# Two 512-token projections in the two banks of one accumulator, and the low tile of the next step made first

## The chip, the core and the metric

The kernel runs on one core of a Trainium2 chip. The metric is device microseconds (us) of one execution, the median over runs. Five engines work side by side and wait for each other through semaphores: TensorE (PE) multiplies matrices into the accumulators of PSUM, VectorE (DVE), ScalarE (ACT) and GpSimd (POOL) work element by element, and SyncE (SP) issues the DMAs.

## The reference

Two layers of a block with three parallel mixers run over 512 latent tokens and 256 context tokens; the context only feeds the latent tokens, and is not updated in the last layer. Cut to what matters:

```python
def _layer(x, ctx, ..., update_ctx):
    h  = _rms_norm(x, norm_g)   * (1.0 + scale)   + shift
    hc = _rms_norm(ctx, norm_g) * (1.0 + scale_c) + shift_c
    (ga_q, ga_k, ga_v, ga_g, ga_lr, hg_q, hg_f, hg_i, hg_g,
     wa_q, wa_k, wa_v, wa_g, mg) = _split_in(jnp.matmul(h, w_in))
    ...                                   # the same columns of hc @ w_in
    y_gla = _head_norm_gate(o_gla, ...)   # chunked recurrence, both directions
    y_hg  = _head_norm_gate(o_hg, ...)    # another one
    y_att = _window_attention(q, k, v, kc, vc, attn_sink) * jax.nn.silu(wa_g)
    x_new = x + gate * _merge((y_gla, y_hg, y_att), mg, w_branch, w_out)
    if update_ctx:                        # layer 0 only
        ctx = ctx + gate_c * _merge(...)
```

`_merge` projects each branch to 1024 columns, weights it with a sigmoid gate, sums the three and multiplies by `w_out`.

## The kernel before

Activations lie transposed, 128 channels to a tile (8 tiles, kt or k), tokens along the columns: 512 latent, then 256 context. Each is split into a rounded high part (hH) and the rest (hL), the weights likewise into WH and WL in a ring `wring` of three slots, and one output block of 128 columns is the sum of WH·hH, WH·hL and WL·hH over the 8 tiles: 24 matmuls of 512 columns, and 24 of 256 where the context is needed (`proj_T`). In layer 0 every projection has both; in layer 1 only keys, forget gates and values need the context, so queries, gates, branch and output projections have 512 columns alone.

A projection's result stands in a tile `acc` of [128, 1024] in PSUM, that is two banks of 512; the pool has two such tiles, taken in turn by `acc()`. Behind the projection an instruction of ScalarE or VectorE reads the tile out (for rotary queries five do: four copies and one product). Smaller results use `mx`, four tiles of one bank.

The recurrences and attention blocks run as background generators. `Emit` keeps an estimated time for each engine, and `pace()` puts background steps between the matmuls of a projection as long as VectorE and ScalarE are less than `SLACK` (3000 ns by its estimate) ahead of TensorE. So what an estimate says of an accumulator (`ps_tile`, `free_at`) decides where background work stands. The order of each engine is the order in which the program records it.

At the very beginning (`j_start`, layer 0) eight rounds k run: `make_h2(k)` makes hL of tile k on VectorE; `products(k, js=(0,))` uses tile k for the first of two projections; `cond_mm(k+2)` multiplies the conditioning weights; `products(k, js=(1,))`; `cond_cols(k+2)` turns the conditioning product by 2-column matmuls into columns, which VectorE adds up; `make_h1(k+2)` scales tile k+2 on VectorE and makes its hH on ScalarE. From round 3 on a weight split for the next job (`split_v`) follows.

Of the kernel before, what the change touches and what calls it, by code (L numbers as in the profile page):

```python
# [28 lines left out]
KT = 8  # L29
NL = 512  # L30
# [289 lines left out]
class Emit:  # L320
# [144 lines left out]
    def stt(self, out, a, s, b, op0, op1):  # L465
        self.nc.vector.scalar_tensor_tensor(out, a, s, b, op0=op0, op1=op1)  # L466
        self._do('v', 1.04 * self.size(out) + 65, out, [a, s, b])
# [5 lines left out]
    def copy(self, out, in_, eng='va', psum=False):  # L473
        n = self.size(out)
        cost = {'v': (1.04 if psum else 0.52) * n + 65, 'a': 0.833 * n + 70, 'g': 3.34 * n + 260}
        cost = {k: c for k, c in cost.items() if k in eng and not (psum and k == 'g')}
        e = self._pick(cost, out, [in_])
        if e == 'v':
            self.nc.vector.tensor_copy(out, in_)  # L479
        elif e == 'a':  # L480
            self.nc.scalar.copy(out, in_)  # L481
        else:
            self.nc.gpsimd.tensor_copy(out, in_)  # L483
        self._do(e, cost[e], out, [in_])
# [47 lines left out]
    def mm(self, out, lhsT, rhs, start=True, stop=True):  # L532
        self.nc.tensor.matmul(out, lhsT=lhsT, rhs=rhs, start=start, stop=stop)  # L533
        n = self.size(rhs)
        if rhs.dtype == F32:
            cost = max(1.667 * n + 6, 224)
        elif rhs.dtype == BF16:
            cost = 60
        else:
            cost = max(0.4167 * n + 13.5, 107 if self.size(lhsT) > 64 else 60)  # L540
        self._do('pe', cost, out, [lhsT, rhs])
# [17 lines left out]
def build(nc, tc, A, COL, es, dump=None):  # L559
# [50 lines left out]
    def ps_tile(kind, p, shape, n):  # L610
        t = p.tile(shape, F32, tag=kind, name=kind)
        names = live[kind]
        if len(names) >= n:
            old = min(names, key=lambda x: E.seq.get(x, 0))
            E.free_at[t.tensor.name] = E.used.get(old, 0.0) + E.FREE
            names.remove(old)
        names.append(t.tensor.name)
        return t

    def mx():  # L620
        return ps_tile('mx', mx_p, [P, 512], 4)

    def acc():
        return ps_tile('acc', acc_p, [P, 1024], 2)


    queue = arena.queue = deque()
# [66 lines left out]
    def pace(slack=SLACK):  # L694
        while max(E.t['v'], E.t['a']) < E.t['pe'] + slack:
            b = first(E.t['pe'] + 50)
            if b is None:
                break
            step(b)
# [91 lines left out]
    def ahead():  # L791

        splits(at_job[0] + NS)

    def WH(i):
        return wring[:, i % NS, 1]

    def WL(i):
        return wring[:, i % NS, 0]

    def proj_T(i, xH, xL, ctx, m=P):

        ps = acc()
        E.t['pe'] = max(E.t['pe'], wready[i])
        for t0, n in ((0, NL), (NL, NC)) if ctx else ((0, NL),):
            k = 0
            for kt in range(KT):
                for w, x in ((WH(i), xH), (WH(i), xL), (WL(i), xH)):
                    mm(ps[0:m, t0:t0 + n], w[:, kt, 0:m], x[kt][:, t0:t0 + n],
                       start=(k == 0), stop=(k == 3 * KT - 1))  # L810
                    k += 1
                if kt == 1 and t0 == 0:
                    ahead()
                if kt % 2 == 1:
                    pace()
        pace()
        return ps
# [114 lines left out]
    def make_h1(l, k, x, r, parts=(0, 1)):  # L932

        for j in parts:
            sl = slice(PARTS[j][0], sum(PARTS[j]))
            stt(x.ap[:, sl], x.ap[:, sl], amod[l][:, k, j:j + 1], r.ap[:, sl], ALU.mult, ALU.mult)
        for j in parts:
            sl = slice(PARTS[j][0], sum(PARTS[j]))
            act(hH[k][:, sl], x.ap[:, sl], AF.Identity, bias=ada[l][:, k, j:j + 1], scale=1.0)

    def make_h2(l, k, x, parts=(0, 1)):

        for j in parts:
            sl = slice(PARTS[j][0], sum(PARTS[j]))
            stt(hL[k][:, sl], x.ap[:, sl], ada[l][:, k, j:j + 1], hH[k][:, sl].bitcast(F32), ALU.add, ALU.subtract)
        if 1 in parts:
            x.free()
# [420 lines left out]
    def split_v():  # L1368
        raw = raw_v.pop(0)
        hl = [arena.alloc(576, True) for _ in range(2)]  # L1370
        E.split(hl[0].r, hl[1].r, raw.ap)
        raw.free()
        S0.setdefault('wvl', []).append([b.r.rearrange("p (a b) -> p a b", b=288) for b in hl] + hl)

    def j_start(l, arg):

        begin_layer(l)
        xs = x_in[l]
# [3 lines left out]
        def load_rest():  # L1382
            for d in range(2):
                nc.sync.dma_start(out=wz_raw[d].ap[0:96], in_=A['wa2'][l][:, d])
            if l > 0:
                return
            S0['mask'] = mb = arena.alloc(6 * P)
            nc.sync.dma_start(out=mb.ap, in_=A['mask'])
            nc.sync.dma_start(out=rot, in_=A['rot'])
# [22 lines left out]
        def cond_mm(k):  # L1412


            w = stage[k]
            ps = mx()
            for kt in range(KT):
                j = kt % 4
                E.mm4(ps[32 * j:32 * j + 32, 0:2 * P], cs32[:, kt], w[kt // 3].ap[:, 256 * (kt % 3):256 * (kt % 3 + 1)],
                      start=(kt < 4), stop=(kt >= 4))  # L1420
            stage[k] = r = arena.alloc(NT)
            copy(r.ap[:, 0:2 * P], ps[:, 0:2 * P], eng='va', psum=True)
            for b in w:
                b.free()

        def cond_cols(k):

            r = stage.pop(k)
            pt = mx()
            for j in range(2):  # L1430
                mm(pt[:, 2 * j:2 * j + 2], r.ap[:, P * j:P * (j + 1)], sel)
            r.free()
            two = ada[l][:, k:16:8]
            tt(two, pt[:, 0:4].rearrange("p (a b) -> p a b", b=2),
               cols_at(f'b_ada{l}', k, 16, 8).unsqueeze(2).to_broadcast([P, 2, 2]), ALU.add)
            stt(amod[l][:, k], ada[l][:, 8 + k], 1.0, col(f'norm_g{l}', k).to_broadcast([P, 2]), ALU.add, ALU.mult)
# [18 lines left out]
        else:  # L1455
            load_rest()
            rs = S0['rs']
            ada_mod(l, 0, 8)
            i = take(2)
        ps = [acc(), acc()]  # L1460
        parts = [((0, NL), (NL, NC)), ((0, NL), (NL, NC))[:2 if S_['ctx'] else 1]]

        def products(kt, of=(0, 1), js=(0, 1)):
            E.t['pe'] = max(E.t['pe'], wready[i + 1])
            for j in js:
                for w, x in ((WH(i + j), hH), (WH(i + j), hL), (WL(i + j), hH)):
                    for t0, n in parts[j]:
                        if (t0 > 0) not in of:
                            continue
                        c = count[j][t0 > 0]  # L1470
                        mm(ps[j][:, t0:t0 + n], w[:, kt], x[kt][:, t0:t0 + n], start=(c == 0), stop=(c == 3 * KT - 1))
                        count[j][t0 > 0] += 1

        count = [[0, 0], [0, 0]]
        if l == 0:

            for k in range(KT):
                make_h2(l, k, xs[k])
                if k == 1:
                    load_rest()  # L1480
                if k == KT - 1:
                    ahead()
                products(k, js=(0,))
                if k + 2 < KT:
                    cond_mm(k + 2)
                products(k, js=(1,))
                if k + 2 < KT:
                    cond_cols(k + 2)
                    make_h1(l, k + 2, xs[k + 2], rs)
                if k >= 3 and raw_v:  # L1490
                    split_v()
        else:

            tail = S0.pop('tail')
            for part in range(2):
                make_h1(l, 0, xs[0], rs, (part,))
                if part == 0:
                    tail[0]()
                for k in range(KT):
                    if k + 1 < KT:  # L1500
                        make_h1(l, k + 1, xs[k + 1], rs, (part,))
                    make_h2(l, k, xs[k], (part,))
                    if part and k == KT - 1:
                        ahead()
                    products(k, (part,))
                    if part == 0 and k in (0, 2):
                        tail[1 + k // 2]()
# [49 lines left out]
    def j_gk(l, h):  # L1557
        ps = proj_T(take(), hH, hL, True)
        S_['k'][h] = kb = arena.alloc(NT)
        copy(kb.ap, ps[:, 0:NT], eng='va', psum=True)  # L1560
# [298 lines left out]
```

## Time and profile before

| what | value |
|---|---|
| median of 3 runs | 2699.06 us (2696.78 to 2701.8) |
| the profiled execution | 2699.6 us, its span 2697.8 us |
| TensorE busy | 2617.0 us, 97% of the span |
| VectorE, ScalarE, GpSimd busy | 1767.1, 1105.6, 168.9 us |
| granted clock of TensorE, mean | 0.991 |
| DMA | 227.68 MB, 84 GB/s |

Busy times are united over an engine's instructions. A matmul's row runs on a little after the next has begun, so rows of TensorE overlap. A bracket behind a row of the timeline gives the idle time before it and the instruction whose end ended it. Names are without numbers: `s` stands for any of 40 slots, `mx` and `acc` for any of the tiles in PSUM. Layer 0 ends near 1540 us.

### The profile page before, as it was taken

To read this page: it belongs to the slowest core of one execution; us is meant where nothing else is said; L and a number is where in the kernel's file an instruction comes from. 1 tells how busy PE (TensorE), PEld (TensorE's weight loads), DVE (VectorE), ACT (ScalarE), POOL (GpSimd) and SP (SyncE) were. 2 spreads that over 40 slices of the span, in tenths; PEclk is the share of its full clock that TensorE was granted. 3 is DMA by queue.
4 is the path that set the end of the run, shared out by engine and by line. 5 is a ranking of instruction groups with operands and counts; after the bars stand their busy time and mean duration, and the time that the engine had idled before them with its cause. 6 is when DMAs were issued, how large, how long until landed. Compare 5 with 4: busy or idle time off the path is not lost. (4 is left out here: it accounts for less than half of the span.)

```text
span 2697.8 us, 40579 instructions
## 1 busy us (share of the span) xinstructions
PE 2617.0 (97%) x15982; PEld 2318.4 (86%) x15982; DVE 1767.1 (66%) x3592; ACT 1105.6 (41%) x2037; POOL 168.9 (6%) x426
## 2 busy tenths in 40 slices
PE   6999999999999999999999999999999999999998
PEld 3899988999888889888888898888899797888886
DVE  4466666786877766775556556667887887765454
ACT  3444434443434455411111344444665545563222
POOL 0000002010020100000000000001011110000000
PEclk8999999999999999999999999999999999999999
DMA  6111121111121112463423411112221122224333
GB/s 251 40 50 57 59 67 59 50 52 57 49 66 50 46 57 74 148 204 101 140 95 102 141 55 56 62 63 63 69 65 62 55 75 73 73 87 142 126 125 109
DMA packets 89342, 227.68 MB, mean 84 GB/s; under 512 B 9920, under 2 KB 30912, under 8 KB 89152
## 3 DMA queue, kind: packets, MB, share of 16 engines
q1 hardware_dynamic: 89152, 225.09, 25.3%
q8 instruction: 126, 2.06, 0.3%
q14 instruction: 64, 0.52, 0.1%
HBM read 202.24 MB, written 22.81 MB: 83 GB/s over the span
## 5 line engine op out<-in xcount | busy, mean ns | idle before, releaser
L533 PE MATMUL acc<-hH,wring 128*128 128x512 f32 (+1 forms) x5040 | 1402.9, 357 | 14.9 <-ACT s L439 9.8
L533 PEld LDWEIGHTS acc<-hH,wring 128*128 128x128 f32 x5040 | 897.7, 190 | 143.1 <-ACT s L439 11.6
L533 PE MATMUL acc<-hL,wring 128*128 128x512 f32 (+1 forms) x2520 | 884.8, 352 | 16.9 <-DVE hL L466 16.8
L533 PEld LDWEIGHTS acc<-hL,wring 128*128 128x128 f32 x2520 | 479.1, 190 | 76.9 <-DVE hL L466 20.5
L533 PE MATMUL mx<-s,s 128*128 128x256 f32 (+4 forms) x2576 | 389.5, 299 | 12.9 <-DVE s L513 4.4
L533 PEld LDWEIGHTS mx<-s,s 128*128 128x128 f32 (+1 forms) x2576 | 348.4, 192 | 32.8 <-issue 7.1
L450 DVE TENSOR_TENSOR wring<-raw,wring 128x1024 fp32r<-128x1024 f32 x269 | 330.7, 1235 | 28.2 <-ACT wring L481 19.3
L533 PE MATMUL acc<-s,wring 128*128 128x512 f32 (+1 forms) x1728 | 332.4, 354 | 0.5 <-DVE s L450 0.5
L533 PEld LDWEIGHTS acc<-s,wring 128*128 128x128 f32 x1728 | 285.6, 189 | 46.4 <-DVE s L450 0.9
L439 ACT ACTIVATE s<-s 128x768 f32<-128x768 f32 (+1 forms) x321 | 259.0, 816 | 129.8 <-DVE s L466 83.1
L481 ACT CAST wring<-raw 128x1024 fp32r<-128x1024 f32 x173 | 179.7, 1048 | 276.9 <-PE acc L533 182.9
L533 PE MATMUL acc<-wring,hH 128*128 128x256 f32 x1536 | 286.1, 285 | 0.0
L450 DVE TENSOR_TENSOR s<-s,s 128x768 f32<-128x768 f32 (+5 forms) x279 | 234.0, 855 | 67.0 <-ACT s L439 45.9
L533 PEld LDWEIGHTS acc<-wring,hH 128*128 128x128 f32 x1536 | 242.2, 192 | 0.3
L533 PE MATMUL acc<-wring,hL 128*128 128x256 f32 x768 | 217.2, 283 | 0.0
L450 DVE TENSOR_TENSOR s<-s,fb 128x128 f32<-128x128 f32 (+2 forms) x608 | 183.0, 361 | 0.8
L439 ACT ACTIVATE s<-acc 128x768 f32<-128x768 f32 (+2 forms) x112 | 76.3, 683 | 255.9 <-PE acc L533 236.2
L481 ACT COPY s<-mx 128x256 f32<-128x256 f32 (+2 forms) x190 | 67.4, 379 | 225.8 <-PE mx L533 142.8
L479 DVE CAST wring<-raw 128x1024 fp32r<-128x1024 f32 x103 | 71.6, 695 | 117.5 <-PE acc L533 114.4
L533 PEld LDWEIGHTS acc<-wring,hL 128*128 128x128 f32 x768 | 147.3, 192 | 0.2
L481 ACT COPY s<-acc 128x768 f32<-128x768 f32 (+2 forms) x129 | 87.8, 681 | 101.0 <-PE acc L533 98.9
L549 PE MATMUL mx<-const,s 128*128 128x128 f32 (+1 forms) x732 | 109.1, 275 | 15.7 <-DVE s L450 14.6
(112 smaller groups left out, 2144.8 us busy)
## 6 DMA issues: line engine op xcount, KB each, us to landing
raw<-in_W SPq DMA_DIRECT2D x308, 512.0 KB, 3.8
y<-s SPq DMA_DIRECT2D x80, 128.0 KB, 1.7
s<-y SPq DMA_DIRECT2D x24, 384.0 KB, 6.1
s<-in_xT SPq DMA_DIRECT2D x16, 384.0 KB, 4.0
s<-in_wada SPq DMA_DIRECT2D x16, 384.0 KB, 7.6
s<-y SPq DMA_DIRECT2D x24, 256.0 KB, 4.4
y<-s SPq DMA_DIRECT2D x80, 64.0 KB, 1.6
s<-in_wvl SPq DMA_DIRECT2D x8, 288.0 KB, 6.2
```

The source lines that it names most:

```text
L439: self.nc.scalar.activation(out, in_, func, **kw)
L450: (self.nc.vector if e == 'v' else self.nc.gpsimd).tensor_tensor(out, a, b, op=op)
L479: self.nc.vector.tensor_copy(out, in_)
L481: self.nc.scalar.copy(out, in_)
L533: self.nc.tensor.matmul(out, lhsT=lhsT, rhs=rhs, start=start, stop=stop)
L549: self.nc.tensor.transpose(out, in_, ident)
```

## The change

`acc_bank()` hands out the first bank of a new `acc` tile and, for the next projection, its second bank, unless two more `acc` tiles have been taken since. `proj_T` uses it for projections without context. And in the rounds of the beginning `make_h2` of tile k+1 is recorded before the second products of tile k, in place of `make_h2(k)` at the head of round k.

```diff
+    half = [None, 0]
+
     def acc():
+        half[1] += 1
         return ps_tile('acc', acc_p, [P, 1024], 2)
+
+    def acc_bank():
+
+        t = half[0]
+        if t is not None and half[1] < 2:
+            half[0] = None
+            return t
+        t = acc()
+        half[:] = t[:, NL:2 * NL], 0
+        return t[:, 0:NL]
...
     def proj_T(i, xH, xL, ctx, m=P):
-        ps = acc()
+        ps = acc() if ctx else acc_bank()
...
+            make_h2(l, 0, xs[0])
             for k in range(KT):
-                make_h2(l, k, xs[k])
                 if k == 1:
                     load_rest()
...
                 products(k, js=(0,))
                 if k + 2 < KT:
                     cond_mm(k + 2)
+                if k + 1 < KT:
+                    make_h2(l, k + 1, xs[k + 1])
                 products(k, js=(1,))
                 if k + 2 < KT:
                     cond_cols(k + 2)
```

The first place is VectorE in the rounds of the beginning (hL_77, hL_78, hL_79 are the low tiles 0, 1, 2; `ada` takes the conditioning columns; s_112 is tile 2 in `make_h1`):

```order
 L466 SCALAR_TENSOR_TENSOR hL_77<-s_110,ada_100,hH_69 128x256
+L466 SCALAR_TENSOR_TENSOR hL_78<-s_111,ada_100,hH_70 128x512
+L466 SCALAR_TENSOR_TENSOR hL_78<-s_111,ada_100,hH_70 128x256
 L450 TENSOR_TENSOR ada_100<-mx,cols 128x2x2
 L466 SCALAR_TENSOR_TENSOR amod_102<-ada_100,cols 128x2
 L466 SCALAR_TENSOR_TENSOR s_112<-s_112,amod_102,s_265 128x512
 L466 SCALAR_TENSOR_TENSOR s_112<-s_112,amod_102,s_265 128x256
-L466 SCALAR_TENSOR_TENSOR hL_78<-s_111,ada_100,hH_70 128x512
-L466 SCALAR_TENSOR_TENSOR hL_78<-s_111,ada_100,hH_70 128x256
+L479 COPY s_378<-mx 128x256
+L466 SCALAR_TENSOR_TENSOR hL_79<-s_112,ada_100,hH_71 128x512
+L466 SCALAR_TENSOR_TENSOR hL_79<-s_112,ada_100,hH_71 128x256
```

Each low tile now stands ahead of the conditioning columns and the next `make_h1`, and from tile 2 on the copy of the conditioning product stands on VectorE in front of it, where ScalarE had it before.

The second place is TensorE between two branch projections of layer 1 (`s` are the split branch outputs, the number behind `acc` tells the tiles apart). Before, each projection has a tile of its own, with a wait at its head:

```order
L533 MATMUL acc_22695<-s1193_22538,wring_85 128x512
L533 MATMUL acc_22695<-s1192_22537,wring_85 128x512
L533 MATMUL acc_22725<-s1157_22273,wring_85 128x512 [waits DVE_49,Activation_49]
L533 MATMUL acc_22725<-s1158_22274,wring_85 128x512
L533 MATMUL acc_22725<-s1157_22273,wring_85 128x512
```

Now the second projection of a pair goes on in the same tile:

```order
L533 MATMUL acc_22673<-s1204_22609,wring_85 128x512
L533 MATMUL acc_22673<-s1203_22608,wring_85 128x512
L533 MATMUL acc_22673<-s1171_22501,wring_85 128x512 [waits DVE_49,Activation_49]
L533 MATMUL acc_22673<-s1172_22502,wring_85 128x512
L533 MATMUL acc_22673<-s1171_22501,wring_85 128x512
```

The matmuls are the same in number and order; the tile is shared, and a wait for VectorE stands in the middle of it. The wait for ScalarE is for the split weights in both. The count behind the wait for VectorE, which the rows don't show, was that of the reader of acc_22665 before, two projections back, and is now that of the reader of acc_22673's first bank, one projection back.

The third place is TensorE at the end of attention, ahead of the first branch projection (mx_22566 is a product of probabilities and values, s1171 the first split branch output). Before, it follows two whole gate projections and half of one more, 60 matmuls with hH and hL:

```order
L533 MATMUL acc_22588<-hL7_84,wring_85 128x512
L533 MATMUL acc_22588<-hH7_76,wring_85 128x512
L533 MATMUL acc_22635<-s1157_22273,wring_85 128x512 [waits DVE_49,Activation_49]
L533 MATMUL acc_22635<-s1158_22274,wring_85 128x512
L533 MATMUL acc_22635<-s1157_22273,wring_85 128x512 [waits DVE_49]
```

Now it follows attention directly:

```order
L533 MATMUL mx_22566<-s1183_22533,s974_19667 128x256 [waits Activation_49]
L533 MATMUL mx_22566<-s1184_22534,s974_19667 128x256 [waits DVE_49]
L533 MATMUL mx_22566<-s1183_22533,s976_19669 128x256
L533 MATMUL acc_22614<-s1171_22501,wring_85 128x512
L533 MATMUL acc_22614<-s1172_22502,wring_85 128x512
```

What moved is the gate projections' place: they stand earlier, and 39 small matmuls of attention stand together behind them.

## Rows read from the trace of the kernel before

**Rows 1.** TensorE's waits, whole span: us in total, times, longest.

```profile
PE acc L533 <- DVE hL L466: 16.8, 8, 3.0
```

**Rows 2.** Timeline of one round of the beginning: start us, us, what [idle before].

```profile
32.15 0.78 PE L533 MATMUL acc<-hL,wring 128*128 128x512 f32 x2 [1.84 <-DVE hL L466]
35.74 0.59 PE L533 MATMUL acc<-hH,wring 128*128 128x512 f32 x2
35.92 0.16 DVE L450 TENSOR_TENSOR ada<-mx,cols 128x4 f32<-128x4 f32 x1 [3.43 <-PE mx L533]
36.31 1.15 DVE L466 SCALAR_TENSOR_TENSOR s<-s,amod,s 128x512 f32<-128x512 f32 x2
37.38 1.14 DVE L466 SCALAR_TENSOR_TENSOR hL<-s,ada,hH 128x512 fp32r<-128x512 f32 x2
38.18 0.97 PE L533 MATMUL acc<-hL,wring 128*128 128x512 f32 x2 [1.84 <-DVE hL L466]
```

**Rows 3.** Chain of work that ended last: start us, us, what.

```profile
2283.75 0.61 ACT s L439
2284.40 2.93 PE acc L533 x6
...
2460.84 114.55 PE acc L533 x504
```

**Rows 4.** Windows: us, busy by engine, PEclk (granted clock), DMA share, GB/s.

```profile
24.70:28.10 3.40, 3.36 (x20) 1.62 (x20) 0.39 (x1) 0.09 (x1) 0.00 (x0) 0.50 1.04 398
1667.50:1675.00 7.50, 7.50 (x36) 6.37 (x37) 6.78 (x11) 1.50 (x3) 0.00 (x0) 1.00 0.39 131
```

**Rows 5.** Timeline, where the first token-major job begins.

```profile
76.65 0.29 PE L533 MATMUL acc<-s,hH 128*128 128x288 f32 x1
```

**Rows 6.** Timeline of the branch projections at the end.

```profile
2466.42 23.96 PE L533 MATMUL acc<-s,wring 128*128 128x512 f32 x105
...
2472.06 0.69 DVE L450 TENSOR_TENSOR s<-s,acc 128x512 f32<-128x512 f32 x1 [3.64 <-PE acc L533]
```

**Rows 7.** Groups of instructions in 2460 to 2690: busy us, mean ns.

```profile
L450 DVE TENSOR_TENSOR s<-s,acc 128x512 f32<-128x512 f32 x24 | 16.5, 688 | 67.8 <-PE acc L533 67.7
L466 DVE SCALAR_TENSOR_TENSOR s<-acc,ada,s 128x512 f32<-128x512 f32 x8 | 6.0, 751 | 18.4 <-PE acc L533 18.4
```

**Rows 8.** Timeline of a pair of the first mixer, layer 1.

```profile
1584.14 0.60 ACT L439 ACTIVATE s<-acc 128x512 f32<-128x512 f32 x1 [2.10 <-PE acc L533]
1584.29 0.40 PE L533 MATMUL acc<-hH,wring 128*128 128x512 f32 x1
```

**Rows 9.** Timeline of three pairs of the middle: first, longest lag, last.

```profile
1845.57 0.62 PE L533 MATMUL acc<-hH,wring 128*128 128x512 f32 x2
1846.44 0.68 DVE L479 COPY s<-acc 128x512 f32<-128x512 f32 x1
...
2274.76 0.48 PE L533 MATMUL acc<-hH,wring 128*128 128x512 f32 x1
2278.62 0.29 ACT L439 ACTIVATE sm<-nsink,sm 128x1 f32<-128x1 f32 x1 [8.58 <-DVE sm L450]
...
2460.20 1.24 ACT L439 ACTIVATE s<-acc 128x512 f32<-128x512 f32 x2
```

**Rows 10.** Waits of VectorE and ScalarE in 2250 to 2450.

```profile
DVE sm L450 <- ACT s L439: 37.2, 32, 2.2
DVE s L450 <- PE mx L533: 7.6, 6, 3.0
...
ACT sm L439 <- DVE sm L450: 49.7, 15, 8.6
ACT s L481 <- PE mx L549: 16.7, 10, 3.2
```

**Rows 11.** TensorE's waits for ScalarE in 2100 to 2455.

```profile
PE acc L533 <- ACT s L439: 7.0, 3, 3.9
```

**Rows 12.** Timeline after a shorter wait of TensorE.

```profile
1667.46 0.74 PE L549 MATMUL mx<-const,s 128*128 128x128 f32 x5 [1.56 <-DVE s L450]
```

## The prediction

> **What bounds the kernel now.** I read the page's busy shares first, then TensorE's waits over the whole span, then the order of both programs, and last the timeline at the places where that order differs. By the shares TensorE is busy nearly all the time (the table above), so an edit pays only where TensorE waits, and costs wherever it makes TensorE wait. The waits give the one big group at the beginning: 16.8 us in 8 waits for the low tile hL [rows 1]. The timeline of one round shows why [rows 2]. VectorE stands idle for 3.43 us until a 2-column product of TensorE ends (35.92), then makes the next tile's first half-step h1 (36.31), and only then hL (37.38); TensorE has stood since 36.33 (35.74 + 0.59) and starts at 38.18. The other place is the end: from 2460.84 on, 504 matmuls take 114.55 us without a pause, 0.227 us each [rows 3]. Nothing there is waited for, so nothing can be won, and a new wait counts in full.
>
> **Part 1, the order of the beginning.** hL of the next tile is now queued on VectorE ahead of that idle time, and its input hH was made a round before. Six of the eight waits go (rounds 1 to 6): three of 1.84 and three of 3.00 us, 14.5 us; that of round 0 stays, and the eighth lies in layer 1. A round without its wait takes 38.18 - 32.15 - 1.84 = 4.19 us. What is late next: the copy of the conditioning product moves from ScalarE to VectorE, in front of hL. From one 2-column product on, VectorE has 0.4 us of small work (35.92 to 36.31), 1.15 of h1, in the last rounds a weight split of 1.2 (what the waits of 3.00 have over those of 1.84), the copy (an estimate of 0.35, half of the 0.69 for 512 columns [rows 7]), and hL of 1.14: 4.3 in all. TensorE asks for hL a round and two hH matmuls later, 4.19 + 0.6 = 4.8: just in time.
>
> The clock could add to it: in 24.7 to 28.1 the granted clock is 0.50, so 1.2 GHz, after such a wait [rows 4]. If every round from 1 on ran at 2.4 GHz, hL of tile 1 would be used at 32.15 - 1.84 = 30.3, that of tile 6 at 30.3 + 5 x 4.19 = 51.3, and the next job would begin after 11 more pairs of matmuls of 768 columns (1.5 x 0.227 = 0.34 us each), at 55.1 instead of 76.65 [rows 5]: 21.5 us. Bounds: -11 (the three short waits stay in half) to -21.5. I take -18, between the waits alone and the whole. TensorE is busy without a gap right after, so the gain carries to the end.
>
> **Part 2, two projections in one accumulator: a new wait.** All projections of layer 1 that have 512 tokens alone now go pairwise into the two banks of one tile; there are 44 pairs. Before, the second one of a pair had a tile of its own. In the order of the changed program the first matmul of every second half has a wait; I followed its count in the program, and each of the 44 points to the ScalarE or VectorE instruction that reads the FIRST half of the same tile. So dependencies go by the tile, not by the bank: the second projection now stands until the first is read out. Queued behind that matmul on TensorE are all others of the projection and, through them, everything. I price it in three stretches.
>
> The end, 20 pairs. The reader starts 0.20 us after the second projection begins (24 x 0.227 after 2466.42 is 2471.87, the reader 2472.06 [rows 6]), takes 0.69 (12 pairs) or 0.75 (4) on VectorE [rows 7] and 0.61 (4) on ScalarE, and a matmul follows its last input by 0.04 us (the read at 2283.75 + 0.61, the matmul at 2284.40 [rows 3]); I take 0.06. So 12 x 0.95 + 4 x 0.87 + 4 x 1.01 = 18.9 us, and no other work of TensorE covers any of it: +18.9.
>
> The first mixer, 4 pairs. Two small matmuls lie between, and the reader ends 1584.14 + 0.60 = 1584.74, where the second projection starts at 1584.29 [rows 8]: 0.51 each with the hop, +2.0.
>
> The middle, 20 pairs between 1845 and 2461. Here the reader is queued behind other work. In the first of them it ends at 1847.12, 1.3 us after the second projection's start at 1845.8 (the second matmul of the row at 1845.57); in the longest, projection two starts at 2274.76 and the reader waits behind a softmax, itself 8.58 us late, until 2283.75 [rows 3, 9]; in the last it ends at 2461.44, 0.6 after the start at 2460.84. The 20 lags with the hop, each taken so, are 1.4, 1.7, 3.6, 5.2, 0.9, 7.9, 4.6, 1.7, 6.8, 9.7, 8.5, 5.8, 5.4, 8.1, 5.4, 2.9, 5.5, 4.4, 1.0 and 0.7: 91 us. That is the upper end, if the readers slip by as much as TensorE does. If they do not slip at all, each stall uses up the lag of the next ones, and a pair costs the longer of its bare latency (0.87 or 0.95; in the 9th, 11th and 14th, where five reads of 0.69 on VectorE empty the tile, 3.65) and its lag less all the stalls before it: 28 us. How much do the readers wait for TensorE? Between 2250 and 2450 VectorE and ScalarE wait 37.2 and 49.7 us for each other in the softmax and only 7.6 and 16.7 for TensorE [rows 10], 22%. So I take a fifth of the way, 28 + 0.2 x 63 = 40.6. Against it, waits of before for a tile still being read go, since the other tile is now always empty by then: 7.0 us [rows 11]. Net +33.6, bounds +14 (28 less these 7, and 7 more under small matmuls in between) and +84.
>
> The recording layer believes that nothing waits, and orders the background work by that. At the end of attention it now leaves 39 small matmuls in one run directly in front of the branch projections, where before 60 large matmuls of gate projections stood between. The last one's chain is then bare: 0 to 12 us (at the longest the 9.6 us from a projection's start to a reader behind such a chain [rows 9], and two or three more); I take 4, under half.
>
> Sum: -18 + 2.0 + 18.9 + 33.6 + 4 = +40.5 us. The profiled execution took 2699.6 (span 2697.8, and 1.8 around it), 0.5 above the median of the runs shown: 2740.1 - 0.5 = 2740.
>
> The trace bears out that two accumulators let the reading of one lie under the next's matmuls, as the reader at 2472.06 does [rows 6]. The Trainium skill (Perfetto Trace Analysis, Matmuls) has a rule for it that speaks for this change: independent groups should rotate through different PSUM banks so that the evacuation of one overlaps the next group. By this rule two banks of one tile are as good as two tiles, and the sum would have no +18.9. Here the wait in the program, not the bank, decides.
>
> **Rivals.** (1) The second halves do not really wait, since the banks differ. Then only part 1 and the 7.0 us of vanished waits are left: 2699 - 18 - 7 = 2674. For it speaks only that no run shows such a wait yet; against it the 44 waits in the order. 0.04. This is the case on the faster side; it decides from the first branch projection on.
> (2) The readers slip with TensorE, the middle costs 84: 2790. For it: the longest lag hangs on a chain that TensorE starts. Against it: the 22%. 0.12.
> (3) The middle is bound by the softmax chain of VectorE and ScalarE anyway, TensorE's stalls use up a lead of up to 9.6 us, and the beginning gains all: -21.5 + 2 + 18.9 + 14 + 0 = +13, 2713. For it: the 87 us that these two wait for each other. 0.17.
> (4) The new gaps lower the clock: six matmuls take 2.93 us after the 3.95 us gap at 2280 [rows 3] against 6 x 0.227 = 1.36, 1.57 more; times 20 pairs at the end, +31: 2771. Against it: after a gap of 1.56 us at 1667 the granted clock is 1.00 [rows 4, 12], and the gaps at the end are 0.95. 0.06. The Trainium skill (TensorE: Matmul & The Clock Gate, section "A second HAM failure mode: psum-queue depth-cycling") describes this mechanism: short idle times between groups of matmuls, frequent enough, make the clock swing between its levels. The trace so far does not agree for gaps this short.
>
> **How the numbers follow.** The forecast holds 0.61, for 2722 to 2765. Range: leaving out most of rival 2 and rival 1 and the lower half of rival 3 gives 2711 to 2780. A difference of 0.2%, 5.4 us, is about what a measurement of this kernel can tell from no change. Faster is rival 1, 0.04; no change needs rival 3 with everything at its lower bound, 0.03; the rest, 0.93, is slower.
>
> **What would show it.** Step 1: waits of acc for hL fall from 16.8 to some 3 us, and the first token-major job begins by 60 us. Step 2: in the last 230 us some 20 new waits of TensorE of 0.9 to 1.0 us for VectorE or ScalarE, each 48 matmuls apart, at a granted clock of 1.00. Middle: 20 waits of acc for ScalarE or VectorE adding up to 28 to 91 us. End of attention: a stretch of some us in which TensorE runs small matmuls alone. The prediction is wrong if the end has no such waits, or if the stretch before 100 us is not shorter by over 10.

## The result, and the profile after

The changed kernel takes 2811.62 us (median; 2808.29 to 2812.21) against 2698.32 for the kernel before in the same comparison: 113 us more, ratio 1.0415, 95% interval 1.0397 to 1.0434. Slower was forecast, but by 40.5 us; the time lies outside the range, above it.

Where do the 113 us come from? Both programs run their 11880 projection matmuls in the same sequence, so the start of one and the same projection can be compared in the two traces, and each stretch shows how far it fell back:

| stretch (times of before) | predicted | after | what it consists of |
|---|---|---|---|
| beginning and layer 0, to 1492.2 | -18 | -20.4 | hL waits gone, clock higher |
| first mixer of layer 1, to 1845.8 | +2.0 | +3.9 | four waits of 0.34, 1.4 in all |
| middle, to 2460.8 | +33.6 | +87.4 | 65.0 idle, 22.4 longer matmuls |
| passage to the branches, to 2471.9 | +4 | +20.4 | the first branch's loads behind the last attention block's stores |
| branch and output projections | +18.9 | +21.2 | 20 waits of 0.69 to 0.94 |
| sum of the spans | +40.5 | +112.6 | |

TensorE's waits after (us in total, times, longest):

```profile
PE acc L533 <- ACT s L439: 53.4, 20, 7.7
PE acc L533 <- DVE s L466: 24.1, 8, 9.1
PE acc L533 <- DVE s L479: 13.0, 4, 6.7
...
PE acc L533 <- ACT s L481: 8.8, 2, 7.2
PE acc L533 <- ACT wring L481: 7.0, 8, 0.9
...
PE acc L533 <- DVE hL L466: 3.5, 6, 1.8
```

The group that led before [rows 1] is the last line now, 3.5 us for 16.8. Above it stand the waits that the change made. The "wring" line is of the same kind. The cast of weights that these eight matmuls wait for in the program had long ended (at 2563.18 for the one at 2575.17 below); another cast just happens to end beside the reader, and the profile names it.

The beginning, one round after the change (start us, us, what):

```profile
34.40 0.42 DVE L479 COPY s<-mx 128x256 f32<-128x256 f32 x1 [0.65 <-PE mx L545]
34.74 1.14 DVE L466 SCALAR_TENSOR_TENSOR hL<-s,ada,hH 128x512 fp32r<-128x512 f32 x2
35.97 0.16 DVE L450 TENSOR_TENSOR ada<-mx,cols 128x4 f32<-128x4 f32 x1
36.22 0.51 PE L533 MATMUL acc<-hL,wring 128*128 128x512 f32 x2
...
56.56 0.40 PE L533 MATMUL acc<-s,hH 128*128 128x288 f32 x1
```

hL is made (34.74) before the column work of the next round (35.97), and TensorE goes on at 36.22 without a wait, where it stood 1.84 us before [rows 2]. The first token-major job begins at 56.56 instead of 76.65 [rows 5].

The middle, windows from the same projection to the same projection. First before, then after (us, busy by engine with the number of records, granted clock):

```profile
1845.80:2460.80 615.00, 595.56 (x3653) 524.92 (x3651) 464.03 (x959) 338.44 (x655) 57.48 (x138) 0.99 0.22 72
```

```profile
1829.30:2531.70 702.40, 617.92 (x3608) 539.87 (x3608) 459.22 (x943) 342.36 (x652) 51.91 (x135) 0.94 0.19 62
2563.10:2800.00 236.90, 219.93 (x940) 174.71 (x940) 103.91 (x128) 49.73 (x62) 2.54 (x2) 1.00 0.32 104
```

TensorE's idle time is the first number less the second: 19.4 us before, 84.5 after, 65.0 more. The 20 new waits alone add up to 80.2 (the first, 1.3 us, ends where the window begins); other waits, 19.0 us before, fell to 5.6. Its busy time grew by 22.4 us, though no matmul was added: the mean granted clock fell from 0.99 to 0.94, and 64 us of the busy time lie at half clock against 7 before. The last row is the tail, with a wait every 12 us and the clock at 1.00.

One of the waits of the middle (after):

```profile
2284.04 2.84 PE L533 MATMUL mx<-s,s 128*128 128x256 f32 x21
...
2286.54 1.77 DVE L517 TENSOR_REDUCE sm<-mx 128x2 f32<-128x512 f32 x3
2288.61 0.29 ACT L439 ACTIVATE sm<-nsink,sm 128x1 f32<-128x1 f32 x1 [3.65 <-DVE sm L450]
2297.25 1.28 ACT L439 ACT_TABLE_LOAD   x1
2298.54 0.60 ACT L439 ACTIVATE s<-acc 128x512 f32<-128x512 f32 x1
2299.19 0.80 PE L533 MATMUL acc<-hH,wring 128*128 128x512 f32 x1 [7.07 <-ACT s L439]
2300.21 1.06 PE L533 MATMUL acc<-hH,wring 128*128 128x512 f32 x2
```

The reader of the first half (2298.54) stands on ScalarE behind two softmax blocks. Their head is VectorE's maximum over the scores (2286.54), and the scores are TensorE's own small matmuls (from 2284.04 on). After 7.07 us TensorE goes on at half clock, 1.2 GHz: two matmuls take 1.06 us instead of 0.62.

The tail (after):

```profile
2574.34 0.69 DVE L450 TENSOR_TENSOR s<-s,acc 128x512 f32<-128x512 f32 x1 [3.35 <-PE acc L533]
2575.17 1.17 PE L533 MATMUL acc<-s,wring 128*128 128x512 f32 x4 [0.87 <-ACT wring L481]
```

As forecast: the reader starts with the end of its projection, ends at 2575.03 (2574.34 + 0.69), and the next matmul follows.

The passage (after):

```profile
2542.58 2.98 PE L533 MATMUL mx<-s,s 128*128 128x256 f32 x22 [0.53 <-DVE s L450]
...
2546.42 0.79 SPq L407 DMA_DIRECT2D y<-s  x2
...
2549.20 0.86 SPq L407 DMA_DIRECT2D y<-s  x2
...
2551.15 2.72 SPq L397 DMA_DIRECT2D s<-y  x4
...
2556.06 1.90 ACT L481 CAST s<-s 128x512 fp32r<-128x512 f32 x3 [10.65 <-DMA s<-y]
2556.73 0.79 PE L533 MATMUL acc<-s,wring 128*128 128x512 f32 x1 [7.19 <-ACT s L481]
```

The last attention block's 22 products run directly in front of the branch projections. SyncE stores attention's results (2546.42, 2549.20) and then issues the loads (2551.15) whose split (2556.06) TensorE waits for, 7.19 us. By the program these loads do not fetch what was just stored: they are the second four tiles of the first branch, written by 1837 us. They are late because they stand in SyncE's queue behind the stores, and the first store waits 18.8 us for attention's product. Before, stores and loads stood in the same order, but the loads went out 12.5 us ahead of the first branch projection (2466.42 [rows 6]):

```profile
2452.97 0.80 SPq L407 DMA_DIRECT2D y<-s  x2
2453.88 1.80 SPq L397 DMA_DIRECT2D s<-y  x4
```

### The profile page after: what moved, and what is told of

It is laid out like the page before. It is cut to its first block, busy times and chain, and to the rows that moved or that the text cites. A ratio compares the mean times of both kernels' runs of the same rounds, so it can differ in the third digit from the quotient of the medians.

```text
span 2810.4 us, 40543 instructions
## 1 busy us (share of the span) xinstructions
PE 2650.7 (94%) x15982; PEld 2336.9 (83%) x15982; DVE 1769.4 (63%) x3594; ACT 1115.4 (40%) x2043; POOL 165.8 (6%) x425
## 5 line engine op out<-in xcount | busy, mean ns | idle before, releaser
L533 PE MATMUL acc<-hH,wring 128*128 128x512 f32 (+1 forms) x5040 | 1427.0, 362 | 92.4 <-ACT s L439 53.4
L533 PEld LDWEIGHTS acc<-hH,wring 128*128 128x128 f32 x5040 | 908.8, 192 | 232.9 <-ACT s L439 60.3
L533 PEld LDWEIGHTS acc<-hL,wring 128*128 128x128 f32 x2520 | 485.4, 193 | 63.6 <-DVE hL L466 5.7
L533 PE MATMUL acc<-s,wring 128*128 128x512 f32 (+1 forms) x1728 | 338.1, 356 | 18.4 <-ACT s L481 7.2
L450 DVE TENSOR_TENSOR s<-s,acc 128x768 f32<-128x768 f32 (+1 forms) x48 | 39.4, 820 | 137.7 <-PE acc L533 137.6
```

Of the source, the lines that this page charges most:

```text
L450: (self.nc.vector if e == 'v' else self.nc.gpsimd).tensor_tensor(out, a, b, op=op)
```

## The experiments

Theories: **W**, the wait of every second half for the reader just before it, with readers that come as late as ever behind their own projection; **O**, the order in which the background is recorded, which the sharing changes too; **K**, the clock that falls in the waits. Times are medians; "before" is 2700.0, 2700.4 and 2702.5 us beside the three groups of runs (1 to 4; 5, 6, 8 and 9; 7, 10 and 11). It was 2698.3 beside the changed kernel, so differences between groups are known to some 4 us.

**1. The beginning alone.** `proj_T` takes `ps = acc()` again.

> The new order of the beginning alone; every projection takes an accumulator tile of its own, as in the kernel before. Theory W (the beginning gains what the start of the second layer showed, and all of the loss is the sharing): the changed kernel reached layer 1 22.0 us earlier, so 2698 - 22 = 2676 us (2673 to 2680). Rival G (the beginning's gain is given back later, by a clock that falls or a load that is then exposed): 2690 to 2700 us. Rival O (part of the loss comes from the order in which the background is recorded, which the sharing changes): says the same as W here.

2678.09 us, ratio 0.9919 (0.9906 to 0.9931): 21.9 faster, and it beats both kernels. The beginning's gain is kept to the end; the sharing costs 133.5 us.

**2. The changed order without the wait.** Every engine's instructions stand as in the changed kernel.

```diff
-            return t
+            u = acc_p.tile([P, 1024], F32, tag='acc', name='acc')
+            ALIAS[u.tensor.name] = t.tensor.name
+            return u[:, 0:NL]
```

(`ALIAS` lets the recording layer go on reckoning with t.)

> The changed kernel, instruction for instruction in the same order on every engine, but the second projection of each pair writes a tile of its own, so it waits for no reader of the first. Theory W (the waits in front of the second halves, and what follows from them, are all of the sharing's cost, the 20.5 us at the end of attention included): 2676 us (2672 to 2682), every wait for an accumulator gone but the 7 us that before had. Rival O (the 20.5 us at the end of attention come from the order of recording): 2693 to 2700 us. Rival C (the middle's half clock comes from the order, not from the waits): 2700 to 2710.

2694.38 us, ratio 0.9976 (0.9967 to 0.9985): rival O. 16.3 of the 133.5 us are the order's, 117.2 the wait's. The middle costs nothing (614.2 us for 615.0), and the passage alone 17.2:

```profile
2446.22 2.98 PE L540 MATMUL mx<-s,s 128*128 128x256 f32 x22 [0.53 <-DVE s L457]
...
2459.39 2.63 ACT L488 CAST s<-s 128x512 fp32r<-128x512 f32 x4 [10.35 <-DMA s<-y]
2460.07 0.79 PE L540 MATMUL acc<-s,wring 128*128 128x512 f32 x1 [6.93 <-ACT s L488]
```

The same late block as after the change, and the same wait behind it, with no shared tile. In the order of before, 15 small matmuls lie in the last three attention and gate projections ahead of it; in this one 114.

**3. Shared tiles, but two back.** The halves are dealt A, B, A, B:

```diff
-        t = half[0]
-        if t is not None and half[1] < 2:
-            half[0] = None
-            return t
+        if len(pend) == 2 and pend[0] is not None:
+            pend[0], t = None, pend[0]
+            return t
+        if len(pend) == 2:
+            t = pend[1]
+            pend.clear()
+            return t
...
+        pend.append(t[:, NL:2 * NL])
```

> The sharing stays, but in the order first half of tile A, first half of tile B, second half of A, second half of B: a second half then waits for the reader of the projection two back, as a tile of its own would. Theory W (what costs is that the reader waited for is that of the projection just before): 2676 us (2672 to 2684). Rival S (what costs is that TensorE writes one bank of a tile whose other bank is being read, or that the tile is waited for as a whole): 2790 to 2812 us, or some 20 us over W if it is a steady contention of 0.5 us a pair.

2680.75 us, ratio 0.9929 (0.9915 to 0.9942): W. 43 pairs share a tile, for 44 in the changed kernel, and it costs 2.7 us over run 1: what counts is which reader a second half waits for. TensorE's waits for ScalarE and VectorE's readers are back at the size of before:

```profile
PE acc L533 <- ACT s L439: 10.0, 7, 2.3
PE acc L533 <- DVE s L466: 3.7, 1, 3.7
```

Dealt so, the rule of the Trainium skill (Perfetto Trace Analysis, section Matmuls) that groups should rotate through banks holds in this trace; with the halves dealt A, A it does not, because the dependency goes by the tile.

**4. The sharing alone.** The beginning as before.

> The sharing alone, with the beginning in the order of before. Theory W (the two edits add up): 2811 + 22 = 2833 us (2828 to 2838). Rival I (they interact: the earlier arrival in layer 1 is what puts loads or readers late): 2811 or less.

2830.18 us, ratio 1.0485 (1.0467 to 1.0503): the edits add up within 5 us (-21.9 and +130.2 against +113.3).

**5. The wait in the order of before.** The counterpart of 2: the recording layer is told of a tile for each projection, while two share one.

```diff
+            ps_tile('acc', acc_p, None, 2, t)
+            return t[:, NL:2 * NL]
```

(Given a tile, `ps_tile` here only notes its second half as one more tile.)

> The counterpart of e8: every engine's instructions in the order of e1 (the beginning alone, 2678 us), but two successive projections share a tile, so each second half waits for the reader of the first. Theory P (the prediction's sizes: readers take over a fifth of TensorE's slip): 2678 + 18.9 + 2.0 + 33.6 + 4 = 2737 us. Theory R (readers slip with TensorE, so the middle costs its 84 in full; no part of the recording order is in it): 2678 + 84 + 21 + 6 = 2789 us (2780 to 2797). Rival N (the wait costs 134 whatever the order, and e8's 16 us are something else): 2805 to 2815.

2804.79 us, ratio 1.0388 (1.0372 to 1.0403): 126.7 over run 1. P is out by 68, R by 16. The time lies at the edge of N's range, but N (the order makes no difference to the wait) does not hold by stretches: against before, the first mixer costs +2.3, the middle +105.2, the passage +1.0 and the tail +21.2, where the changed kernel has 87.4 in the middle and 20.4 in the passage. (Run 1's own middle takes 618.3 us, 3.3 more than before's.) The middle:

```profile
1821.40:2541.70 720.30, 626.02 (x3653) 545.17 (x3653) 464.98 (x958) 338.70 (x656) 57.42 (x138) 0.93 0.19 61
```

94.3 us idle, 74.8 more than before: nearly the 84 of full slip. The 20 waits add up to 91.1 us, the 91 of the prediction's list; older waits fell from 19.0 us to 4.0, where the prediction took 7.0 off. The other 30.5 are longer matmuls, which R had left out. This order is that of before, so each reader can be set beside itself. In the middle's pair with the longest lag, before:

```profile
2272.49 0.39 PE L533 MATMUL acc<-hH,wring 128*128 128x512 f32 x1
...
2276.71 1.61 DVE L517 TENSOR_REDUCE sm<-mx 128x2 f32<-128x512 f32 x3
```

and here:

```profile
2282.04 0.39 PE L541 MATMUL acc<-hH,wring 128*128 128x512 f32 x1
...
2286.38 1.61 DVE L525 TENSOR_REDUCE sm<-mx 128x2 f32<-128x512 f32 x3
...
2288.29 0.29 ACT L447 ACTIVATE sm<-nsink,sm 128x1 f32<-128x1 f32 x1 [8.57 <-DVE sm L458]
...
2293.42 0.60 ACT L447 ACTIVATE s<-acc 128x512 f32<-128x512 f32 x1
2294.07 0.80 PE L541 MATMUL acc<-hH,wring 128*128 128x512 f32 x1 [9.57 <-ACT s L447]
```

From the projection's last matmul to the reader it was 11.26 us before (2272.49 to 2283.75 [rows 3]) and is 11.38 here, and ScalarE's wait for the softmax is 8.57 for 8.58 [rows 9], although TensorE was by then 31 us later in its work than run 1's (9.6 us behind before for 21.2 ahead). Of the 59 projections of the middle that have 512 columns, 50 have a reader that starts within 0.15 us of its lag before; the mean lag is 4.13 us for 4.32. Of the 20 first halves that a second half waits for, 18 are read out within 0.15 us of their old lag. The readers slip in full.

**6. Sharing in the mixers and attention alone.**

```diff
+        share[0] = l == 1 and name not in ('yload', 'mg', 'yneed', 'br', 'out')
```

> The changed kernel, but the 40 branch and output projections and the last gates beside them take a tile each; the mixers and the attention share as in the change. Theory R (the stretches add up, the tail's 20 pairs cost the 21.2 us that their starts fell back by): 2811.6 - 21.2 = 2790 us (2787 to 2794). Rival: the tail's waits cost nothing by themselves, since the output's readers end the kernel anyway: 2805 or more.

2764.37 us (1.0219 to 1.0253), 26 under the expectation. By the starts the branch and output projections cost 0.0 here for 21.2, as expected. Of the other 26, 23 lie in the last gates (middle 75.2 for 87.4) and the passage (9.4 for 20.4), which I had counted to the mixers; the rest lies in the stretch to 1492.2, whose program is the same.

**7. Sharing in the last gates and the tail alone**, the complement.

> The beginning's new order, and the sharing in the last gates and the branch and output projections alone (the complement of em). Theory A (the stretches add up: after - em = 47.2): 2678.1 + 47 = 2725 us (2720 to 2730). Rival B (of these 47, the 20 at the passage from attention to the first branch come about only when the mixers share too, since the order of recording there is theirs): 2678.1 + 21 = 2699 us (2696 to 2707).

2718.34 us (1.0045 to 1.0075), 40.2 over run 1: nearest to A, 1.7 under its range, and 11 above B's. Its tail costs 21.3, the gates and the passage 17.4.

**8, 9. The reader right behind its projection,** with and without sharing. In a projection without context, `proj_T` hands out background work in its first half only:

```diff
-                if kt % 2 == 1:
+                if kt % 2 == 1 and (ctx or kt < 4):
                     pace()
-        pace()
+        if ctx:
+            pace()
```

> The changed kernel, but in layer 1 no background work is recorded in the second half of a projection or at its end, so the reader of its accumulator stands in its engine's queue with little ahead of it. Read against e6n, which records in the same way without sharing. Theory Q (a wait is as long as the work that is queued ahead of the reader; with none, the bare way over, 1.06 us a pair as in the tail): e6 - e6n = 44 x 1.06 = 47 us (40 to 65). Rival X (the reader comes late because the chain of the softmax that stands ahead of it is itself late, wherever background is recorded): 90 to 134 us.

> The control of e6: the same recording rule, a tile for each projection. Recording less background ahead may starve VectorE and ScalarE: 2678 us if it costs nothing, up to 2750 if it does. Both theories say the same here; it is the base that e6 is read against.

2754.05 and 2692.39 us: the wait costs 61.7 instead of 117.2, inside Q's range. By stretches it is 3.2, 36.7, 0.2 and 22.7. The middle, with and without sharing:

```profile
1822.80:2449.60 626.80, 586.64 (x3490) 515.13 (x3490) 444.20 (x902) 319.20 (x593) 51.09 (x134) 0.97 0.21 66
```

```profile
1820.50:2410.70 590.20, 573.97 (x3492) 507.43 (x3490) 441.80 (x902) 318.95 (x593) 51.62 (x134) 0.99 0.22 71
```

The 20 waits of the middle add up to 29.4 us here, for 80.2 in the changed kernel. So what is queued ahead of a reader sets most of a wait in the middle. The second row is 28 us shorter than run 1's middle (618.3), but its passage takes 54.6 us for 11.0: the postponed attention work stands there. That is why this rule alone doesn't beat run 1.

**10. The waits filled.** Seven to 37 matmuls that nobody reads stand ahead of the 15 second halves with the longest waits, with all else in the order of the change.

```diff
+            n = FILL.get(pair[0], 0)
+            if n:
+                f = mx_p.tile([P, 512], F32, tag='mx', name='fill')
+                for _ in range(n):
+                    nc.tensor.matmul(f, lhsT=hH[0][:, 0:P], rhs=hH[0][:, 0:512], start=True, stop=True)
```

> The changed kernel in the same order, with extra matmuls (7 to 37 of 128x512, into a tile that nobody reads) ahead of the 15 second halves that waited 2.4 us or more in the middle, so many that they end about 0.6 us before the reader does. TensorE then stays busy in these waits, and the waits stay as long. Theory K (some 27 us of the loss are the clock that falls to half after the waits: 64.4 + 9.7 us busy at half clock against 13.6 + 5.7 in e8): 2811.6 - 27 = 2785 us (2778 to 2795), hardly any half clock between 1829 and 2563 us. Rival L (the readers' chains set the pace there, and TensorE's clock is lost beside them): 2805 to 2818 us at full clock.

2781.84 us (1.0279 to 1.0309), 29.8 under the changed kernel: K. One filled wait, and the middle's window:

```profile
2279.70 3.56 PE L641 MATMUL fill<-hH 128*128 128x512 f32 x15
2283.90 0.50 PE L533 MATMUL acc<-hH,wring 128*128 128x512 f32 x1 [0.64 <-ACT s L439]
```

```profile
1823.50:2498.30 674.80, 654.94 (x3893) 571.74 (x3893) 459.53 (x943) 342.31 (x652) 52.57 (x135) 1.00 0.19 64
```

The clock stands at 1.00 for 0.94, and the stretch is 27.6 us shorter. The waits are as long as they were; only what came behind them is faster.

**11. The recording layer told of the wait.**

```diff
             half[0] = None
+            E.t['pe'] = max(E.t['pe'], E.used[t.tensor.name] + E.FREE)
             return t
```

> The changed kernel, but the recording layer is told of the wait: its clock of TensorE is moved to the time it reckons for the first half's reader before the second half is recorded, so it places background work by that. Theory U (the loss is partly that the order is planned for a wait that it doesn't know of): 2770 to 2795 us. Rival T (telling it moves the background, not the reader, which still stands behind the work recorded before it): 2800 to 2820 us.

2770.24 us, ratio 1.0255 (1.0238 to 1.0272), 41.4 under the changed kernel: U. The middle costs 71.3 for 87.4, the passage 0.9 for 20.4. Planning with the wait takes away the bare passage and a part of the waits; it is still 92 us behind run 1.

## Why the prediction was wrong

**The beginning was right** in its mechanism, and the sum took it a little low: -21.9 measured for -18, at the bound of -21.5 that stood for full clock. From 20 us to the first token-major job, 6.8 us lie at half clock for 20.5 before.

**The tail was right**: +21.2 for +18.9, 20 waits, clock 1.00. The waits that the profile shows add up to 16.6; the other 4.6, some 0.2 us a pair, are for the most part the overlap of matmuls that each wait breaks (a row takes 0.39 us, but without a wait the next begins 0.23 us after it), which the sum had left out. The first mixer's +2.0 came out as 2.3 (run 5) and 3.9; its four waits are 0.34 each, where 0.51 was taken.

**The step that failed is the fifth of the way** in the middle: "Between 2250 and 2450 VectorE and ScalarE wait 37.2 and 49.7 us for each other in the softmax and only 7.6 and 16.7 for TensorE [rows 10], 22%. So I take a fifth of the way". A wait is put down to its last releaser. ScalarE's 8.58 us for VectorE [rows 9] are a link in a chain whose head, the maximum over mx, can't start before TensorE's scores. The waits inside that chain are its length, not its freedom: they are long, and they begin when TensorE says. Run 5 shows it reader by reader: the lags stayed, so stalls use up no lead, and the 20 lags come due whole, as waits of 91.1 us; net of the older waits that went, TensorE stands 74.8 us longer, where the prediction had 33.6. The changed kernel obeys the same rule in its own order: in run 2, where nothing waits, the 20 lags, taken as the prediction takes them, are 80.2 us, and its 20 waits are 80.2. This was rival 2's mechanism, which had 0.12.

**A second term was missing:** the clock was weighed for the tail alone (rival 4), where the gaps were too short to lower it, and not for the middle, where the prediction's own list had lags up to 9.7 us, and [rows 3, 11] a slow stretch behind a wait of 3.95. It is worth 22.4 us in the middle by the rows and 29.8 by run 10 with the passage. Rivals 2 and 4 were taken as alternatives; they came together, the one's mechanism in the other's place, and the range ended at 2780, short of rival 2 alone.

**The end of attention, +4,** was seen (a run of small matmuls bare in front of the branches) and mis-sized: 20.4, of which run 2 gives 17.2 to the order alone. It was bounded by one softmax chain of 9.6 us, as if the branch waited for attention's result. What it waits for are its own loads, in SyncE's queue behind the stores of that result; the gates that covered them before now come ahead of the attention work. The orders don't simply add, though: with the waits, the changed order costs the whole kernel 6.8 us against run 5, without them 16.3 against run 1.

Rival 1, that the second halves do not wait, is out (run 3 shows when it would hold); so is rival 3, that the softmax chain hides the stalls.

What stays open: why the sharing moves the recorder's order just so, and which of its moves make run 11's 41 us; neither was taken apart.

## What to carry to other kernels

Before two results share a tile, ask by what the dependencies go: here by the tile, so the next user of it must be the one two back, not the next one. To price a new wait for a reader, take the reader's lag behind its own producer as fixed, unless the chain ahead of it can be shown to start without that producer; waits of two engines for each other are no such proof. Where the wait is long, add the clock behind it, and look in the new order for a store that now comes late and for the loads queued behind it.

## What the runs showed of the hardware

Behind which waits TensorE's granted clock falls was not as clean as expected. In the changed kernel's middle, 1.32, 1.48 and, at 2439.7, 2.58 us of idle left it at 1.00, while 2.37 us at 2341.3 were followed by 0.50 within 2 us; that one came 19 us behind the end of another stretch at half clock. Each of the 13 waits of second halves there that were 3.0 us or longer had a stretch at 0.50 beside or behind it. In the tail, 20 waits of 0.69 to 0.94 us, one every 12 us, never lowered it. The Trainium skill (TensorE: Matmul & The Clock Gate, section "A second HAM failure mode: psum-queue depth-cycling") says that frequent short idle times between groups make the clock swing; at this spacing no run here shows that. In run 10, what was left of the filled waits (0.6 to 1.4 us) kept the clock up: work whose result nobody reads bought 29.8 us.
